# Six z_a and two z_b column blocks moved into block-product pairs, with index scores summed by adding DMAs, deferred low parts and ScalarE norm squares

## The chip, the cores and the metric

The kernel runs on one core of a Trainium2 chip. The metric is the device time of one execution in microseconds (us). The kernel before takes 1558.45 us, the median of 3 runs (1557.06 to 1560.39).

## The reference, cut to what matters

One layer of a hybrid block on 16 meta tokens and 512 tokens (528 columns), width 2048, all in fp32:

```python
proj = rms_norm(x, norm_g) @ w_in
q_a, k_a, v_a, z_a, q_i, k_i, w_i, q_b, f_b, i_b, z_b, gates = split(proj)
# branch A: index scores pick 128 keys per query, attention over these
score = einsum('bqhs,bqh->bqs', relu(qi @ ki), w_i)      # 16 index heads
sel   = top_k(where(admissible, score, -inf), 128)
o_a   = softmax(q @ k[sel] * d**-0.5) @ v[sel]           # 8 heads; q, k normed and rotated
y_a   = o_a * silu(z_a)
# branch B: gated linear recurrence over 8 heads
o_b   = hgrn2(silu(q_b), 1 - f, i_b, log(f))             # f from sigmoid(f_b)
y_b   = rms_norm(o_b) * silu(z_b)
# merge
out = x + sum_n(sigmoid(gates_n) * (y_n @ w_branch_n)) @ w_out
```

## The kernel before, in words

Activations lie transposed: 128 channels on the partitions, tokens along the row. An fp32 product is three fp32r matmuls on TensorE (PE): both factors are split into a high and a low part, and hi·hi, lo·hi and hi·lo are summed (`mm3`, and L90 and L92 in `mm`).

The projection is cut into column blocks of 128 channels. A **plain block** runs over 16 k tiles, 3 matmuls of 128x512 each: 48 matmuls into one PSUM bank, `pg`. A **pair** (`run_pair`) computes two blocks at once over four quarters of the weights (11, 12, 21, 22) and two halves of tokens, by seven block products instead of eight (`SEVEN`): each product has 8 k tiles and 3 matmuls of 256 columns (264 where meta tokens are needed), into the banks px, py, pz, pw. That is 7 x 24 = 168 matmuls for two blocks. The sums of weights for a pair are made by VectorE (DVE; `sum_1`, `sum_2`) and by two adding DMAs on GpSimd's queue (POOL; `sum_3`, `sum_4`, L115). The combinations of the products are made by DVE in p1, g1 and g2.

The order of blocks is the list `jobs`: k_i with w_i; 8 q_i; 8 z_a; 4 k_a; 4 v_a; 8 q_a; 6 z_b: 39 plain blocks. Then 29 pairs: 5 with q_b and the last two z_b, 8 of f_b with i_b (264 wide), 16 of gates. Then 32 blocks of the branch matmul (24 matmuls 128x512 each, and 768 in all for both branches' halves), then 8 pairs of the output matmul. The blocks of one kind hang together with tasks: 8 `idx_task` make the scores of 16 index heads (PE `psc`, relu on ScalarE (ACT) into `rl`, weighted sum on DVE, L127); 4 `topk_task` find the 128 largest by 16 rounds of MAX8 and MATCH_REPLACE8 (L682, L683); `ka_task`, `va_task` and `qa_task` norm, rotate and attend; `pv_task` ends a head and multiplies it by silu(z_a), read back from HBM (zad); `hgrn_task` runs one head of the recurrence at a time.

**What sets the order.** The program is written in the order in which Python issues it. A clock per engine is modelled (`Core.at`); between the main matmuls `pump` lets waiting tasks issue their next piece when the model says that what they wait for is there. Each engine then runs its own instructions in that order, and waits at the first one whose operands aren't there.

**Weights.** Each chunk of 1024 columns is loaded on SyncE's queue (SP, L362) into one of NRAW = 6 `raw` buffers, split by ACT (`wh`, L100) and DVE (`wl` = raw - wh, L106) into one of 3 buffers each, two chunks ahead of PE (`split_upto`). Both halves of the split are issued together in `hi_lo`; the load that refills a raw buffer is issued behind the last use of that buffer.

Of the kernel before, what the change touches and what calls it, by code (L numbers as in the profile page):

```python
# [37 lines left out]
LAT = 180.0  # L38
ROOM = 2
SAME = {"pe": 0.0, "act": 60.0, "dve": 125.0, "pool": 60.0}  # L40
MARGIN = 300.0
NSLOT = 69


class Core:
# [67 lines left out]

    def dma_add(self, out, a):
        self.nc.gpsimd.dma_start(out, a, accum_op=OP.add)  # L115
        return self.at("pool", 4000.0, [out], [out, a])
# [27 lines left out]
class Slots:  # L144
# [36 lines left out]
def hybrid_kernel(ctx, tc, x, meta, vecs, w_in, rows, w_branch, w_out,  # L181
# [64 lines left out]
    def bank(name):  # L246
        while len(B1.free) <= need[0]:
            yield WAIT
        return B1.get(name)

    def pair(name, keep=0):
        while len(B2.free) <= keep:
            yield WAIT
        return B2.get(name)
# [37 lines left out]
    masks = cp.tile([128, 7 * 256 + 512], U8, name="masks")  # L292
# [8 lines left out]
    def make_masks():  # L301
        mf = slot("mf")
        nc.sync.dma_start(mf[:, :448], masks_d)
        yield E.clk["pe"] + 3000.0
        for i in range(7):
            yield E.dve([masks], [mf], 256, lambda v: v.tensor_copy(
                masks[:, 256 * i:256 * i + 256].rearrange("p (c n) -> p c n", c=4),
                mf[:, None, 64 * i:64 * i + 64].to_broadcast([128, 4, 64])))
        yield E.dve([masks], [ident], 512, lambda v: v.tensor_copy(
            masks[:, 1792:2304].rearrange("p (c n) -> p c n", c=4), ident[:, None, :].to_broadcast([128, 4, 128])))  # L310
        S.put(mf)

# [39 lines left out]
    NRAW = 6  # L352
# [27 lines left out]
    def hi_lo(k, src, m):  # L380
        h = wp.tile([128, 1024], F32R, name=f"wh{k}", tag=f"wh{k % NWS}")
        l = wp.tile([128, 1024], F32R, name=f"wl{k}", tag=f"wl{k % NWS}")
        E.act(h[:, :m], src, AF.Copy)
        (E.ptt if k < 6 else E.tt)(l[:, :m], src, h[:, :m].bitcast(F32), OP.subtract)
        return h, l

    def split_chunk(k, ch):
        load_upto(ch["i"])
# [3 lines left out]
        if k < 4:  # L392
            for g in range(2):
# [19 lines left out]
    def sum_2(pr):  # L413
        if not hasattr(pr, "s2"):
            pr.s2 = wp.tile([128, 1024], F32, name=f"sum2_{pr.raw['11']['i']}", tag="s2")
            E.tt(pr.s2, pr.s1, pr.raw["11"]["raw"], OP.add)

    def sum_3(pr):
        if not hasattr(pr, "s3"):
            pr.s3 = pr.raw["21"]["raw"]  # L420
            E.dma_add(pr.s3, pr.raw["11"]["raw"])

    def sum_4(pr):
        if not hasattr(pr, "s4"):
            pr.s4 = pr.raw["12"]["raw"]
            E.dma_add(pr.s4, pr.s2)

    def prep_op(k, op):

        pr, nm = op["pair"], op["name"]  # L430
        first = pr.raw["11"]["i"]
        load_upto(first + (0 if nm == "11" else 2 if nm == "s2" else 3))
# [7 lines left out]
        h, l = hi_lo(k, src, 1024)  # L440
# [3 lines left out]
        used = {"s3": 2, "22": 3, "s4": 4}.get(nm)  # L444
        if used:
            load_upto(first + used - 1 + NRAW)

# [84 lines left out]
    def norm_rope(ps, p, ntab, tab, name):  # L532
# [6 lines left out]
        E.act(sv, ps, AF.Square)  # L539
        E.red(r[:, 0:4], sv)  # L540
# [3 lines left out]
        E.tt(yv, ps, r[:, 8:12, None].to_broadcast([p, 4, 128]), OP.mult)  # L544
# [13 lines left out]
    def ki_task(kw):  # L558
# [45 lines left out]
        for c0, n, v in ((0, 272, pb[:, 0, :272]), (272, 256, pb[:, 1, :256])):  # L604
            E.act(kkH[:, c0:c0 + n], v, AF.Copy)
            E.tt(kkL[:, c0:c0 + n], v, kkH[:, c0:c0 + n].bitcast(F32), OP.subtract)
        S.put(d, dm)
        B2.put(pb)
        kk.extend((kkH, kkL))

    score = []
    idx_left = [8]

    def idx_task(j, xq):
# [18 lines left out]
        if not score:  # L633
            score.extend(slots("score", 4))
        for i in range(2):
            hd = 2 * j + i
            for qt in range(4):
                kq = KQ[qt]
                lq = st_[i][:, 128 * qt:128 * qt + 128]
                if kq > 512:  # L640
                    pb = yield from pair("psc")
                    for c in range(2):
                        E.mm(pb[:, c, :264], lq, kkH[:, 264 * c:264 * c + 264], True, False)
                        e = E.mm(pb[:, c, :264], lq, kkL[:, 264 * c:264 * c + 264], False, True)
                    v = pb[:, :, :264]
                else:
                    pb = yield from bank("psc")
                    E.mm(pb[:, :kq], lq, kkH[:, :kq], True, False)
                    e = E.mm(pb[:, :kq], lq, kkL[:, :kq], False, True)
                    v = pb[:, :kq]  # L650
                yield e
                r = slot("rl")
                rv = r[:, :kq].rearrange("p (a b) -> p a b", a=2) if kq > 512 else r[:, :kq]
                E.act(rv, v, AF.Relu)
                (B2 if kq > 512 else B1).put(pb)
                sc = score[qt][:, :kq]
                w = wi[:, qt, hd:hd + 1]
# [15 lines left out]
    def topk_task(qt):  # L673
        kq = KQ[qt]
        sc = score[qt][:, :kq]
# [12 lines left out]
        S.put(ws, score[qt])  # L688
# [77 lines left out]

    zad = [tc.dram_tile([128, 512], F32, name=f"zad{h}") for h in range(8)]
    yd = [[tc.dram_tile([128, 512], F32, name=f"yd{n}_{h}") for h in range(8)] for n in range(2)]

    def spill(dst, s, e):  # L770
        yield e
        nc.sync.dma_start(dst, s[:, :512])
        S.put(s)

# [3 lines left out]
    def qa_task(h, xq, prev):  # L778
# [46 lines left out]
        for qt in (3, 2, 1, 0):  # L825
            kq = KQ[qt]
            xs = ps[qt] = slot("lg")
# [17 lines left out]
    def pv_task(h, ps, e):  # L845
# [10 lines left out]
        def turn(b):  # L856
# [6 lines left out]
            if b >= 0 and b < 3:  # L863
# [7 lines left out]
        for b in (3, -1, 0, 1, 2):  # L871
# [33 lines left out]
        e = E.tt(z[:, :512], po, z[:, :512], OP.mult)  # L905
        B1.put(po)
        spawn(spill(yd[0][h], z, e), 0)
# [11 lines left out]
    MT = cp.tile([128, 256], F32, name="MT")  # L919
    VM = [cp.tile([128, 16], F32, name=f"VM{i}") for i in range(2)]  # L920
    LB = []

    def lb_task():
        while not all(t.done for t in qa_tasks):
            yield WAIT
        LB.append((yield from pair("phl")))
        E.dve([LB[0]], [], 512, lambda v: v.memset(LB[0][:, 0], 0.0))

    def hgrn_task(h, prev):
# [6 lines left out]
        while not LB:  # L936
            yield WAIT
        while len(S.free) < 3:
            yield WAIT
        at = AT[0]  # L940
        mt, vt = MT, slot("vt")
        pm = LB[0][:, 1, :]
        pb = yield from bank("phv")
        E.tr(pm[:16, :128], VM[h % 2], ident)
# [13 lines left out]
        E.dve([at], [pb], 512, lambda v: v.copy_predicated(at[:, :512], masks[:, 1792:2304], pb))  # L958
# [5 lines left out]
        for li, m in enumerate(LEVELS):  # L964
            pb = LB[0][:, 0, 256 * (li % 2):256 * (li % 2) + 256]
# [4 lines left out]
            for c in range(4):  # L970
# [164 lines left out]
    def d_fb(h):  # L1135
        def f(g):
# [578 lines left out]
```

## Time and profile before

| | us |
|---|---|
| median of the runs | 1558.45 |
| the profiled execution | 1557.17 |
| its span, first to last instruction | 1555.4 |
| PE busy | 1536.8 (99%) |
| DVE busy | 1102.3 (71%) |
| ACT busy | 635.0 (41%) |
| POOL busy | 135.1 (9%) |
| the 16 DMA engines, queue q1 and q0 | 38.9% and 14.8% of the span |

Busy time is that of the profiled execution. A share of the whole span says little about one stage: the stages differ, and the views by window below give them apart. In the chain of work that ended last, each piece is followed back from the end of the program to what released it; what stands there is what the time is made of. In the views of single instructions the first two columns are the start and the duration in us, and the bracket is the idle time of the engine just before, with what ended it.

### The profile page before, as it was taken

To read this page: it belongs to the slowest core of one execution; us is meant where nothing else is said; L and a number is where in the kernel's file an instruction comes from. 1 tells how busy PE (TensorE), PEld (TensorE's weight loads), DVE (VectorE), ACT (ScalarE), POOL (GpSimd) and SP (SyncE) were. 2 spreads that over 40 slices of the span, in tenths; PEclk is the share of its full clock that TensorE was granted. 3 is DMA by queue.
4 is the path that set the end of the run, shared out by engine and by line. 5 is a ranking of instruction groups with operands and counts; after the bars stand their busy time and mean duration, and the time that the engine had idled before them with its cause. 6 is when DMAs were issued, how large, how long until landed. Compare 5 with 4: busy or idle time off the path is not lost.

```text
span 1555.4 us, 29048 instructions
## 1 busy us (share of the span) xinstructions
PE 1536.8 (99%) x11904; PEld 1417.1 (91%) x11904; DVE 1102.3 (71%) x1903; ACT 635.0 (41%) x997; POOL 135.1 (9%) x136
## 2 busy tenths in 40 slices
PE   7999999999999999999999999999999999999998
PEld 6888889998888799999999999999999888889998
DVE  6687898625677888677677767686767544778775
ACT  5555422334445453443444344434433332334332
POOL 3100000100000001101000000100000000002222
PEclk9999999999999999999999999999999999999999
DMA  9323343333223465766757676757666755448773
GB/s 261 82 68 82 108 115 109 83 82 86 84 82 109 117 156 129 181 153 155 178 144 170 150 171 149 170 138 175 153 173 159 234 177 149 136 137 219 210 209 93
DMA packets 293173, 223.00 MB, mean 143 GB/s; under 512 B 10356, under 2 KB 264832, under 8 KB 293040
## 3 DMA queue, kind: packets, MB, share of 16 engines
q1 hardware_dynamic: 275664, 173.88, 38.9%
q0 software_dynamic: 10720, 38.89, 14.8%
q10 hardware_dynamic: 6656, 8.39, 1.6%
q8 instruction: 93, 1.52, 0.4%
q14 instruction: 40, 0.33, 0.1%
HBM read 161.35 MB, written 20.97 MB: 117 GB/s over the span
## 4 chain that ended last, share of the span: by engine, by line
PE 96%; ACT 1%; DVE 1%; DMA 1%; issue 1%; POOL 0%; ACTq 0%; SPq 0%; DVEq 0%; POOLq 0%
PE pg L92 39%; PE pz L90 11%; PE py L90 11%; PE px L90 10%; PE po L90 10%; PE pw L90 5%; PE phl L92 1%; PE psc L92 1%; PE pho L92 1%; PE pov L90 1%; PE plg L92 1%; PE ppt L96 1%; PE phs L92 1%; PE px L96 1%; PE pqa L96 0%
## 5 line engine op out<-in xcount | busy, mean ns | idle before, releaser
L100 ACT ACTIVATE wh<-raw 128x1024 fp32r<-128x1024 f32 x291 | 308.4, 1060 | 485.2 <-PE pg L92 128.8
L106 DVE TENSOR_TENSOR wl<-raw,wh 128x1024 fp32r<-128x1024 f32 x289 | 356.7, 1234 | 191.9 <-ACT wh L100 188.6
L92 PE MATMUL pg<-hH,wh 128*128 128x512 f32 (+1 forms) x720 | 261.1, 363 | 0.0
L92 PE MATMUL pg<-hH,wl 128*128 128x512 f32 (+1 forms) x720 | 256.1, 356 | 0.0
L92 PE MATMUL pg<-hL,wh 128*128 128x512 f32 (+1 forms) x720 | 255.9, 355 | 0.0
L90 PE MATMUL po<-wh,mh 128*128 128x256 f32 x896 | 158.7, 280 | 0.5 <-DVE xq L106 0.5
L92 PEld LDWEIGHTS pg<-hH,wl 128*128 128x128 f32 x720 | 135.3, 188 | 21.0
L92 PEld LDWEIGHTS pg<-hH,wh 128*128 128x128 f32 x720 | 135.7, 189 | 16.6
L92 PEld LDWEIGHTS pg<-hL,wh 128*128 128x128 f32 x720 | 135.4, 188 | 16.0
L90 PEld LDWEIGHTS po<-wh,mh 128*128 128x128 f32 x896 | 137.7, 189 | 0.8 <-DVE xq L106 0.7
L100 ACT ACTIVATE wh<-sum 128x1024 fp32r<-128x1024 f32 x74 | 78.5, 1061 | 140.0 <-PE pw L90 52.2
L90 PE MATMUL px<-hH,wh 128*128 128x256 f32 (+1 forms) x464 | 134.3, 289 | 0.0
L90 PE MATMUL px<-hH,wl 128*128 128x256 f32 (+1 forms) x464 | 130.8, 282 | 0.0
L90 PE MATMUL px<-hL,wh 128*128 128x256 f32 (+1 forms) x464 | 130.5, 281 | 0.0
L90 PE MATMUL po<-wl,mh 128*128 128x256 f32 x448 | 125.9, 281 | 0.0
L106 DVE TENSOR_TENSOR wl<-sum,wh 128x1024 fp32r<-128x1024 f32 x74 | 96.7, 1307 | 33.4 <-ACT wh L100 33.3
L92 PE MATMUL pg<-yH,wh 128*128 128x512 f32 x256 | 101.0, 394 | 0.0
L92 PE MATMUL pg<-yH,wl 128*128 128x512 f32 x256 | 100.8, 394 | 0.0
L92 PE MATMUL pg<-yL,wh 128*128 128x512 f32 x256 | 100.6, 393 | 0.0
L90 PEld LDWEIGHTS px<-hH,wh 128*128 128x128 f32 x464 | 87.4, 188 | 0.6
L90 PEld LDWEIGHTS px<-hL,wh 128*128 128x128 f32 x464 | 87.3, 188 | 0.0
L90 PEld LDWEIGHTS px<-hH,wl 128*128 128x128 f32 x464 | 87.3, 188 | 0.0
(312 smaller groups left out, 3368.5 us busy)
## 6 DMA issues: line engine op xcount, KB each, us to landing
raw<-in_w_in_dram SPq DMA_DIRECT2D x192, 512.0 KB, 4.2
raw<-raw POOLq DMA_DIRECT2D x37, 512.0 KB, 5.3
raw<-sum POOLq DMA_DIRECT2D x37, 512.0 KB, 6.1
raw<-in_w_branch_dram SPq DMA_DIRECT2D x32, 512.0 KB, 4.5
raw<-in_w_out_dram SPq DMA_DIRECT2D x32, 512.0 KB, 4.3
gd<-g SPq DMA_DIRECT2D x32, 256.0 KB, 4.6
g<-gd SPq DMA_DIRECT2D x30, 256.0 KB, 2.9
x<-in_x_dram SPq DMA_DIRECT2D x16, 256.0 KB, 5.4
```

The source lines that it names most:

```text
L90: self.nc.tensor.matmul(out, lhsT, rhs, start=start, stop=stop, skip_group_check=True)
L92: self.nc.tensor.matmul(out, lhsT, rhs, start=start, stop=stop)
L96: self.nc.tensor.transpose(out, in_, ident)
L100: self.nc.scalar.activation(out, in_, f, **kw)
L106: self.nc.vector.tensor_tensor(out, a, b, op=op)
```

## The change

The numbers of plain z_a and z_b blocks become 2 and 4 (`NZA`, `NZB`). The other 6 z_a and 2 z_b go into pairs with the q_b, so that 31 plain blocks and 33 pairs are left. Heads 2 to 7 of the attention end before their z_a is there: `pv_task` copies o_a and stores it to HBM (`oad`), and a new `ya_task` loads it and multiplies when the pair with z_a is done.

The index heads' products are scaled on ACT in place, the relu of query tiles 1 and 0 is one instruction, and the heads are summed by 45 adding DMAs on POOL's queue into the tiles of head 0. In `norm_rope` (k_a, their meta columns, q_a) the squares are four ACT instructions with an accumulator and the scaling is four ACT instructions.

The low part of a split is no longer issued with the high part: `low()` waits in `lows`, and `flush` issues it when the model says that ACT's copy is done, or when the next products need it. NRAW goes from 6 to 5, and the number of 528-column work slots from 69 to 72. The recurrence's masks move from buffers of their own into one slot, `p1` in a pair goes away (g1 and g2 are combined in place), the reciprocals of a softmax become one instruction, and model costs of DMAs change.

```diff
+NZA, NZB = 2, 4
...
-NSLOT = 69
+NSLOT = 72
...
     def dma_add(self, out, a):
         self.nc.gpsimd.dma_start(out, a, accum_op=OP.add)
-        return self.at("pool", 4000.0, [out], [out, a])
+        e = self.at("pool", 1000.0, [out], [out, a]) + 4000.0
...
+    lows = []
+
+    def flush(k):
+
+        while lows and (lows[0][1] <= E.clk["pe"] or lows[0][0] <= k):
+            lows.pop(0)[2]()
+
     def pump(limit=3000.0):
+        flush(-1)
...
-    NRAW = 6
+    NRAW = 5
...
-        E.act(h[:, :m], src, AF.Copy)
-        (E.ptt if k < 6 else E.tt)(l[:, :m], src, h[:, :m].bitcast(F32), OP.subtract)
+        def low():
+            (E.ptt if k < 6 else E.tt)(l[:, :m], src, h[:, :m].bitcast(F32), OP.subtract)
+            load_upto(upto)
+
+        lows.append((k, E.act(h[:, :m], src, AF.Copy), low))
+        if k < 6:
+            flush(k)
         return h, l
 
     def split_chunk(k, ch):
+        flush(k - 2)
...
-        E.act(sv, ps, AF.Square)
-        E.red(r[:, 0:4], sv)
+        for b in range(4):
+            E.act(sv[:, b], ps[:, b], AF.Square, accum_out=r[:, b:b + 1])
...
-        E.tt(yv, ps, r[:, 8:12, None].to_broadcast([p, 4, 128]), OP.mult)
+        for b in range(4):
+            e = E.act(yv[:, b], ps[:, b], AF.Copy, scale=r[:, 8 + b:9 + b])
+        yield e
...
+                for qt in qts:
+                    e = E.act(r[:, o:o + KQ[qt]], r[:, o:o + KQ[qt]], AF.Copy, scale=wi[:, qt, hd:hd + 1])
+                    if hd == 0:
+                        score[qt] = r[:, o:o + KQ[qt]]
+                    o += KQ[qt]
                 if hd == 0:
-                    e = E.ts(sc, r[:, :kq], w, None, OP.mult)
+                    sums[qts] = r
                 else:
-                    e = E.stt(sc, r[:, :kq], w, sc, OP.mult, OP.add)
-                S.put(r)
+                    yield e
+                    E.dma_add(sums[qts][:, :o], r[:, :o])
+                    S.put(r)
...
+    def ya_task(h, s):
+
+        while h not in have_o or not S.free:
+            yield WAIT
+        o = slot("oa")
+        nc.sync.dma_start(o[:, :512], oad[h])
+        yield E.clk["pe"] + 5000.0
+        e = E.tt(o[:, :512], o[:, :512], s[:, :512], OP.mult)
+        S.put(s)
+        spawn(spill(yd[0][h], o, e), 0)
+        yield e
...
-        e = E.tt(z[:, :512], po, z[:, :512], OP.mult)
+        if h < NZA:
+            e = E.tt(z[:, :512], po, z[:, :512], OP.mult)
+            spawn(spill(yd[0][h], z, e), 0)
+        else:
+            e = E.act(z[:, :512], po, AF.Copy)
+            spawn(spill(oad[h], z, e, lambda: have_o.add(h)), 0)
...
+    for t in "iiiiiiiiaakkkkvvvvqqqqqqqqbbbb":
+        c, m, d = kinds[t]
+        jobs.append(Job("in", c + 128 * count[t], 128, m, done=d(count[t])))
...
-    Q, Z = ([(c + 128 * h, d(h)) for h in range(8)] for c, d in ((C_QB, d_qb), (C_ZB, d_zp)))
-    first = [(Z[6], Q[0]), (Z[7], Q[1]), (Q[3], Q[2]), None, (Q[5], Q[4]), None, (Q[7], Q[6]), None]
+    blocks2 = [(h, (C_QB + 128 * h, d_qb(h))) for h in range(8)]
+    blocks2 += [(h + 0.8, (C_ZB + 128 * h, d_zp(h))) for h in range(NZB, 8)]
+    blocks2 += [(0.4 + 6.0 * (h - NZA) / (8 - NZA), (C_ZA + 128 * h, d_zap(h))) for h in range(NZA, 8)]
+    blocks2.sort(key=lambda b: b[0])
```

The score sums on POOL's queue, at the start of the program. `rl` are the products of an index head (528 columns for query tile 3, 400 for tile 2, 416 for tiles 1 and 0 together), `kay` and `kis` the norms, `raw`, `wh` and `wl` the first chunks of the weights. In before:

```order
L110 TENSOR_TENSOR wl_740<-raw_215,wh_739 128x1024
L566 MEMSET kiy_803 128x320
L110 TENSOR_TENSOR kis_804<-kis_804,mhalf 128x5
L110 TENSOR_TENSOR kay_2587<-kay_2587,mhalf 128x4
L110 TENSOR_TENSOR kay_2735<-kay_2735,mhalf 128x4
```

The same place in after:

```order
L603 MEMSET kiy_796 128x320
L111 TENSOR_TENSOR kis_797<-kis_797,mhalf 128x5
L121 DMA rl_955<-rl_977 128x528
L121 DMA rl_955<-rl_999 128x528
L121 DMA rl_969<-rl_1002 128x400
L121 DMA rl_969<-rl_1024 128x400
L121 DMA rl_983<-rl_1045 128x416
L121 DMA rl_983<-rl_1064 128x416
```

POOL had nothing between the norm of k_i and that of k_a; it now has the adding DMAs, 15 into each of three tiles, one behind the other.

DVE where the first top-k begins, in after (`rl_983` holds the scores of tiles 1 and 0, `zs` is silu(z_a) of a plain block, `wl` the low part of a chunk):

```order
L107 TENSOR_TENSOR wl_1820<-raw_1496,wh_1819 128x1024
L107 TENSOR_TENSOR wl_1873<-raw_1575,wh_1872 128x1024
L718 MEMSET rl_983 64x64
L724 MAX m_0_1894<-rl_983 128x8
L725 MATCH_REPLACE tk_1893<-m_0_1894,rl_983 128x144
L107 TENSOR_TENSOR zs_1912<-pg_1818,zs_1912 128x512
L107 TENSOR_TENSOR wl_1918<-raw_1628,wh_1917 128x1024
L107 TENSOR_TENSOR wl_1972<-raw_1696,wh_1971 128x1024
```

In before, DVE's own sums of the scores (L127) stand ahead of that place:

```order
L106 TENSOR_TENSOR wl_1498<-raw_1120,wh_1497 128x1024
L127 SCALAR_TENSOR_TENSOR score_942<-rl_1521,tabs_98,score_942 128x144
L127 SCALAR_TENSOR_TENSOR score_943<-rl_1530,tabs_98,score_943 128x272
L127 SCALAR_TENSOR_TENSOR score_944<-rl_1539,tabs_98,score_944 128x400
L127 SCALAR_TENSOR_TENSOR score_945<-rl_1550,tabs_98,score_945 128x528
L106 TENSOR_TENSOR wl_1560<-raw_1176,wh_1559 128x1024
```

The score sums are gone from DVE; the MEMSET of `rl_983` waits for the last adding DMA into it, and the `wl` of the next chunks stand behind that MEMSET.

DVE in a pair of f_b and i_b, in before, from the low part of its s3 product to that of its s4 product (with numbers; `raw82` to `raw85` are the buffers of this pair, `raw86` to `raw88` and `sum1_86` belong to the next):

```order
L106 TENSOR_TENSOR wl88_5839<-raw83_5421,wh88_5838 128x1024
L106 TENSOR_TENSOR hz_444_5847<-g1_440_5681,hz_444_5847 128x512
L106 TENSOR_TENSOR p1_443_5837<-p1_443_5837,py_232_5850 128x264
L106 TENSOR_TENSOR wl89_5879<-sum1_82_5708,wh89_5878 128x1024
L106 TENSOR_TENSOR wl90_5907<-raw84_5599,wh90_5906 128x1024
L106 TENSOR_TENSOR p1_443_5837<-py_232_5850,p1_443_5837 128x264
L106 TENSOR_TENSOR sum1_86_5939<-raw87_5714,raw88_5842 128x1024
L106 TENSOR_TENSOR wl91_5942<-raw85_5601,wh91_5941 128x1024
```

The same place of a pair of f_b and i_b in after (`raw66` to `raw69` are its buffers, `raw70` to `raw72` the next pair's; `oa` is o_a of an attention head, `zs` silu(z_a)):

```order
L107 TENSOR_TENSOR wl72_5332<-raw67_5100,wh72_5331 128x1024
L107 TENSOR_TENSOR g1_408_5368<-g2_406_5330,py_208_5343 128x264
L107 TENSOR_TENSOR wl73_5372<-sum1_66_5200,wh73_5371 128x1024
L107 TENSOR_TENSOR oa_405_5307<-oa_405_5307,zs_404_5299 128x512
L107 TENSOR_TENSOR wl74_5401<-raw68_5102,wh74_5400 128x1024
L107 TENSOR_TENSOR g2_406_5330<-py_208_5343,g2_406_5330 128x264
L107 TENSOR_TENSOR sum1_70_5433<-raw71_5339,raw72_5341 128x1024
L107 TENSOR_TENSOR wl75_5436<-raw69_5173,wh75_5435 128x1024
```

The order in a pair stays, but for the multiplication of `oa`. With five raw buffers `raw72` takes the buffer of `raw67`, so that its load stands behind `wl72`, five instructions ahead of `sum1_70`, which reads it; in before `raw88` takes the buffer of `raw82`, which the adding DMA of s3 reads last, ahead of `wl88`.

## Rows read from the trace of the kernel before

**Rows 1.** The page of the profile: busy time of each engine, the granted clock of PE in 40 slices, and the chain of work that ended last, by engine.

```profile
PE 1536.8 (99%) x11904; PEld 1417.1 (91%) x11904; DVE 1102.3 (71%) x1903; ACT 635.0 (41%) x997; POOL 135.1 (9%) x136
...
PEclk9999999999999999999999999999999999999999
...
PE 96%; ACT 1%; DVE 1%; DMA 1%; issue 1%; POOL 0%; ACTq 0%; SPq 0%; DVEq 0%; POOLq 0%
```

**Rows 2.** The waits of PE over the whole span, the first two and the last of nine rows (14.7 us in all): line waited for, us in total, times, longest.

```profile
PE pc L96 <- DMA vrow<-in_vecs_dram: 8.2, 1, 8.2
PE phs L92 <- ACT MT L100: 2.6, 8, 1.3
...
PE pov L90 <- DVE pTL L106: 0.2, 1, 0.2
```

**Rows 3.** ACT's timeline: the first instruction behind three of the eight z_a blocks, the second being the next block and the third six blocks behind the first.

```profile
174.62 0.60 ACT L100 ACTIVATE zs<-pg 128x512 f32<-128x512 f32 x1 [0.65 <-PE pg L92]
...
185.86 0.60 ACT L100 ACTIVATE zs<-pg 128x512 f32<-128x512 f32 x1 [4.76 <-PE pg L92]
...
242.06 0.60 ACT L100 ACTIVATE zs<-pg 128x512 f32<-128x512 f32 x1 [4.80 <-PE pg L92]
```

**Rows 4.** The chain of work that ended last, pieces in order of time (start, us, what): the first and the last product of a 256-wide pair, the first of the pair behind it, and the branch matmul.

```profile
553.28 2.85 PE px L90 x24
...
570.30 2.83 PE pz L90 x24
573.14 2.92 PE px L90 x24
...
1214.86 177.81 PE pg L92 x768
```

**Rows 5.** Windows of the stages: index scores; z_a blocks; k_a and v_a; attention; the pair of rows 4; two pairs and a head of the recurrence. Columns: us, then busy us and count of PE, PEld, DVE, ACT and POOL, granted clock of PE, DMA share, GB/s.

```profile
70.00:165.00 95.00, 95.00 (x478) 80.73 (x477) 72.33 (x120) 52.56 (x98) 0.00 (x0) 1.00 0.27 73
174.00:242.00 68.00, 68.00 (x293) 54.65 (x292) 64.80 (x184) 15.63 (x18) 0.00 (x0) 1.00 0.45 124
254.00:356.00 102.00, 102.00 (x793) 98.58 (x793) 51.36 (x95) 34.98 (x78) 6.46 (x7) 1.00 0.31 83
356.00:553.00 197.00, 195.44 (x1003) 161.94 (x1002) 143.94 (x358) 92.69 (x182) 9.32 (x9) 1.00 0.35 95
553.00:573.00 20.00, 20.00 (x171) 19.95 (x170) 17.09 (x26) 11.81 (x20) 1.74 (x2) 1.00 0.77 172
594.00:664.00 70.00, 68.62 (x730) 67.04 (x729) 51.63 (x82) 27.97 (x40) 6.17 (x7) 1.00 0.66 158
```

**Rows 6.** Groups of instructions of the parts that the change edits: xcount, busy us, mean ns of one, idle before and its releaser.

```profile
L127 DVE SCALAR_TENSOR_TENSOR score<-rl,tabs,score 128x144 f32<-128x144 f32 (+3 forms) x60 | 32.1, 564 | 13.0 <-ACT rl L100 12.8
L682 DVE MAX8 m<-tk 128x8 f32<-128x144 f32 (+3 forms) x60 | 30.1, 502 | 0.0
L683 DVE MATCH_REPLACE8 tk<-m,tk 128x144 f32<-128x144 f32 (+3 forms) x60 | 29.5, 492 | 0.0
L106 DVE TENSOR_TENSOR wl<-raw,wh 128x1024 fp32r<-128x1024 f32 x289 | 356.7, 1234 | 191.9 <-ACT wh L100 188.6 <-DMA raw<-in_w_in_dram 1.5 <-DMA yd<-za 1.2
L132 DVE TENSOR_REDUCE qay<-qas 128x4 f32<-128x512 f32 x8 | 5.4, 677 | 1.1 <-ACT qas L100 1.1
L106 DVE TENSOR_TENSOR qay<-pqa,qay 128x512 f32<-128x512 f32 x8 | 5.5, 686 | 1.2 <-POOL qay L110 1.1
L100 ACT ACTIVATE rl<-psc 128x400 f32<-128x400 f32 (+3 forms) x64 | 27.2, 451 | 38.8 <-PE psc L92 38.6
L100 ACT ACTIVATE qas<-pqa 128x512 f32<-128x512 f32 x8 | 4.7, 589 | 1.7 <-PE pqa L96 1.7
L100 ACT ACTIVATE v<-pva 128x128 f32<-128x128 f32 x4 | 1.1, 277 | 5.6 <-DVE vL L106 5.6
L100 ACT ACTIVATION_READ_ACCUMULATOR lg<-lg,small 128x1 f32 x32 | 6.0, 187 | 0.0
L115 POOL DMA_DIRECT2D raw<-raw x37 | 31.9, 862 | 533.2 <-DVE sum L106 533.2
```

**Rows 7.** PE's timeline, the starts of the first matmuls of two successive q_i blocks, each with score matmuls behind it; and the page's list of DMA issues (KB each, us to landing).

```profile
139.24 4.88 PE pg L92 x21
...
153.06 4.89 PE pg L92 x21
...
raw<-in_w_in_dram SPq DMA_DIRECT2D x192, 512.0 KB, 4.2
raw<-raw POOLq DMA_DIRECT2D x37, 512.0 KB, 5.3
```

**Rows 8.** DVE's and SP's timeline and the chain in one 264-wide pair: the low part of the pair's s3 product, the load issued behind it, the sum for the next pair, the low part of its s4 product, and that product on PE.

```profile
758.09 1.23 DVE L106 TENSOR_TENSOR wl<-raw,wh 128x1024 fp32r<-128x1024 f32 x1 [1.08 <-ACT wh L100]
...
759.34 0.37 SPq L362 DMA_DIRECT2D raw<-in_w_in_dram  x1
...
766.20 1.21 DVE L106 TENSOR_TENSOR sum<-raw,raw 128x1024 f32<-128x1024 f32 x1
767.34 1.22 DVE L106 TENSOR_TENSOR wl<-raw,wh 128x1024 fp32r<-128x1024 f32 x1
...
771.65 2.92 PE pz L90 x24
```

More of the change, by code (lines that the diff above doesn't have):

```diff
@@ L164, in get, with when @@
         return a
+    def when(self):
+        return min(self.last[t][0] for t in self.free) + LAT
     def put(self, *aps):
@@ L246, in bank @@
     def bank(name):
-        while len(B1.free) <= need[0]:
+        while len(B1.free) <= need[0] or B1.when() > E.clk["pe"]:
             yield WAIT
@@ L251, in pair @@
     def pair(name, keep=0):
-        while len(B2.free) <= keep:
+        while len(B2.free) <= keep or B2.when() > E.clk["pe"]:
             yield WAIT
@@ L439, in prep_op @@
             src = {"s1": pr.s1, "s2": pr.s2, "s3": raw["21"], "s4": raw["12"]}[nm]
-        h, l = hi_lo(k, src, 1024)
+        used = {"s3": 2, "22": 3, "s4": 4}.get(nm, 0)
+        h, l = hi_lo(k, src, 1024, first + used - 1 + NRAW if used else -1)
         w = pr.ncols
@@ L632, in idx_task @@
         kkH, kkL = kk
-        if not score:
-            score.extend(slots("score", 4))
         for i in range(2):
             hd = 2 * j + i
[L637 to L650, printed above, removed]
+            for qts in ((3,), (2,), (1, 0)):
+                pb = yield from (pair if qts == (3,) else bank)("psc")
+                o = 0
+                for qt in qts:
+                    kq = KQ[qt]
+                    lq = st_[i][:, 128 * qt:128 * qt + 128]
+                    for c, n in ((0, 264), (1, 264)) if kq > 512 else ((0, kq),):
+                        out_ = pb[:, c, :n] if kq > 512 else pb[:, o:o + n]
+                        E.mm(out_, lq, kkH[:, n * c:n * c + n], True, False)
+                        e = E.mm(out_, lq, kkL[:, n * c:n * c + n], False, True)
+                    o += kq
@@ L687, in topk_task @@
         e = E.ts(bias[qt], w, BIAS, None, OP.mult)
-        S.put(ws, score[qt])
+        S.put(ws)
+        if qt > 1:
+            S.put(sums[qt,])
+        elif all(t.done for t in topk_tasks[:2] if t is not topk_tasks[qt]):
+            S.put(sums[1, 0])
         yield e
@@ L826, in qa_task @@
             kq = KQ[qt]
-            xs = ps[qt] = slot("lg")
+            xs = ps[qt] = slot("lg") if qt else ps[1][:, KQ[1]:KQ[1] + kq]
             f2 = (lambda a: a.rearrange("p (a b) -> p a b", a=2)) if kq > 512 else (lambda a: a)
@@ L925, in lb_task @@
             yield WAIT
-        LB.append((yield from pair("phl")))
-        E.dve([LB[0]], [], 512, lambda v: v.memset(LB[0][:, 0], 0.0))
+        lb = yield from pair("phl")
+        E.dve([lb], [], 512, lambda v: v.memset(lb[:, 0], 0.0))
+        LB.append(lb)
     def hgrn_task(h, prev):
@@ L935, in hgrn_task @@
         q, f, k, vx = (hg[h][i] for i in ("q", "f", "k", "v"))
-        while not LB:
+        while len(LB) < 2:
             yield WAIT
+        masks = HC[3]
         while len(S.free) < 3:
@@ L940, in hgrn_task @@
         at = AT[0]
-        mt, vt = MT, slot("vt")
-        pm = LB[0][:, 1, :]
+        mt, vt = HC[0], slot("vt")
+        lb = next(t for t in LB if t != 1)
+        pm = lb[:, 1, :]
         pb = yield from bank("phv")
-        E.tr(pm[:16, :128], VM[h % 2], ident)
+        E.tr(pm[:16, :128], HC[1 + h % 2], ident)
         for c in range(4):
@@ L1154, in f @@
         def f(g):
-            E.act(VM[h % 2].rearrange("p (a b) -> p a b", a=2), halves(g)[:, :, 0:8], AF.Copy)
+            if h == 0:
+                spawn(hgrn_consts(), 0)
+                while not HC:
+                    pump(1e9)
+            E.act(HC[1 + h % 2].rearrange("p (a b) -> p a b", a=2), halves(g)[:, :, 0:8], AF.Copy)
             hg[h]["v"] = g
@@ L1161, in f, with d_zap @@
             s = silu_mul(b, "hz")
-            hg.setdefault(h, {})["z"] = 1
-            spawn(spill(zd[h], s, E.clk["dve"] + LAT), 0)
+            spawn(spill(zd[h], s, E.clk["dve"] + LAT, z_there(h)), 0)
+        return f
+    def d_zap(h):
+        def f(g):
+            s, _ = silu(g, "zs")
+            spawn(ya_task(h, s), 1)
         return f
```

145 lines of the change are left out of this document (84 added, 61 removed).

## The prediction, before the run

> **What bounds the kernel now.** I read the page first: PE is busy 99% of the span, at the full granted clock in every slice, and 96% of the chain that ended last lies on PE [rows 1]. So the time is the sum of PE's matmuls and the few places where PE stands still. The waits of PE are 14.7 us in all, of which 8.2 come before the first matmul, so 6.5 us lie within the program [rows 2]. Then the windows by stage: DVE is at 95% beside the z_a blocks (64.80 of 68.00), and PE is nevertheless busy for the whole window; in the attention PE loses 1.56 us of 197 at 73% of DVE, and in two pairs with a head of the recurrence 1.38 of 70 [rows 5]. A stage can therefore be nearly full on DVE without any cost, as long as the order is right. What the change is worth is read from PE's work first, then from what new waits it makes.
>
> **Fewer matmuls.** Eight plain blocks (8 x 48 matmuls) go and four pairs (4 x 168) come. A plain block's price: from the first silu behind a z_a block to that six blocks on, 242.06 - 174.62 = 67.44 us, 11.24 each, or 234 ns per 512-wide matmul [rows 3]; PE is full there and holds little but these [rows 5]. A pair's: 573.14 - 553.28 = 19.86 us, or 118 ns per 256-wide matmul [rows 4]. So 8 x 11.24 = 89.9 us go and 4 x 19.86 = 79.4 come: **-10.5 us**. The branch matmul gives a second price, 177.81 / 768 = 231.5 ns [rows 4], 11.11 a block, and with it -9.4. I take the z_a blocks' own price, since they are what goes.
>
> The Trainium skill ("TensorE: Matmul & The Clock Gate", "Back-to-back issue gap") gives a sustained spacing of 81 ns at 128 columns and 131 ns at 512. By an estimate from it a block is 48 x 131 = 6.3 us, a pair at some 95 ns 16.0, and the change would add 4 x 16.0 - 8 x 6.3 = 13.6 us. The trace differs, with 234 and 118 ns at the full granted clock [rows 1, 3, 4]: here halving the columns halves the time, so I give this rule 1 in 100.
>
> **New pairs' other work.** Each needs two sums on DVE, and two adding DMAs and their issue on POOL. The pair of rows 4 has all this and PE is busy 20.00 of 20.00 us [rows 5]: 0. Loading and multiplying o_a adds one DVE instruction to six pairs, of 0.69 us by the nearest 512-wide row (`qay`) [rows 6]; DVE has 2.9 us free in such a pair [rows 5]: 0, and at most 6 x 0.69 = 4.1 if no gap were found.
>
> **The score stage.** DVE loses its sums, 60 x 0.564 us and a few more. ACT gains 64 scalings; priced like the relus, 27.2 us [rows 6], that makes 52.56 + 27.2 = 79.8 of 95 us, 84% [rows 5]. PE is the engine it serves, with the high parts and the relus; as DVE served at 95% elsewhere, I take 0. POOL, idle there [rows 5], gets 45 issues x 0.862 = 38.8 us [rows 6]. The adds into one tile follow each other at the pace of heads: two heads per q_i block, 153.06 - 139.24 = 13.82, so 6.91 us a head; a 512 KB adding DMA lands in 5.3 us [rows 7] and these are half as large. So the sums keep up, and the last is there at most 3 x 0.862 + 5.3 = 7.9 us behind the last product. The first MEMSET of the top-k waits for it, with silu(z_a) and the next two `wl` queued behind it on DVE; the two `wl` ahead of it hold PE busy for one block, 11.24 us. 0, with 3.3 us to spare.
>
> **k_a, v_a and attention.** The top-k (30.1 + 29.5 = 59.6 us of DVE [rows 6]) loses six z_a blocks as its cover and runs beside two of them and the k_a and v_a. Estimate of DVE there: 64.80 + 51.36 [rows 5], less 12 `wl` at 1.234, 6 silu products at 0.686 and 5 norms at 0.677 + 0.686 [rows 6], so 116.2 - 25.8 = 90.4 us in 68 + 102 - 67.4 = 102.6, 88%. It was 95% without loss, but without chains in which PE waits for DVE's results; k_a and v_a have them. The norms on ACT: four squares with their accumulator reads and four scalings, 4 x (0.277 + 0.187) + 4 x 0.277 - 0.589 = 2.4 us more on ACT and 1.36 less on DVE each [rows 6], 13 times. ACT has two thirds of that stage free [rows 5]; the chain of one norm gets longer by about 1 us, which delays what waits on it in a task and not PE, which meanwhile has main matmuls. The attention has two z_b blocks fewer beside it, and its DVE share stays: (143.94 - 8 x 1.36 - 4 x 1.234) / (197 - 22.5) = 73%. Cost of the thinner cover, bounded by the nearest rows: all 6.5 us of waits within the program [rows 2] could go (-6.5), and the k_a and v_a could lose what the pairs with a head lose, 2% (1.38 of 70), some +2, or several times that. I take **+1**, since nothing of the old waits is touched.
>
> **Five raw buffers and late low parts.** The load that the next pair's `sum1` reads now waits for the low part of s3. In one pair that ends at 759.32 and the issue stands at 759.34 [rows 8]; with a landing of 4.2 us [rows 7] the data are there at 763.5; the sum starts at 766.20: 2.7 us to spare, and the low part of s4 behind it ends 3.1 us before its product (768.56 against 771.65) [rows 8]. So 0. The deferred low parts fill idle time of DVE, of which 188.6 us stand in front of `wl` waiting for ACT [rows 6]; as DVE isn't the bound, 0 too. Masks, reciprocals, p1 and the slot number touch only DVE and memory: 0.
>
> **The sum**, against the profiled execution's 1557.17: 1557.17 - 10.5 + 1.0 = 1547.7. The median of the runs, 1558.45, stands 1.3 above it, so the forecast for the median is **1549.0**, in its own range of 1545 to 1553.5 (below: 3 us of the old waits gone and none new; above: the cheaper block price and 3.5 us more of new waits).
>
> **Rivals.**
> - *A thin cover (0.15).* Top-k pieces stand in front of what the k_a and v_a chains need, and PE, in order, waits at their transposes. For it: DVE goes from 50% to an estimated 88% there [rows 5]. Against it: the modelled clocks place the tasks, and at 95% nothing was lost. Eight tasks with some three hand-overs each, every one late by one MAX8 of 0.5 us [rows 6], make 12 us at the most and half of it likely, on top of the forecast: 1554 to 1561.
> - *Sums that don't keep up (0.06, slower).* If an adding DMA takes longer than a head's 6.91 us, the lag grows 15 times, and DVE stands at the top-k's MEMSET with the `wl` behind it. With t per add PE loses about 15 x (t - 6.91) + t + 1.7 - 11.2. It decides against the change from t = 7.9 us (13 us lost); at 8 us, 1564. Against it are the 5.3 us for twice the bytes [rows 7]; for it, that three tiles' adds share POOL's queue with an issue of 0.86 us each. The Trainium skill ("SBUF — State Buffer", "SBUF: two separate sides") says that a DMA issued from GpSimd can't write its descriptors while VectorE holds the port that they share, and tells of 620 ns becoming 3100. By it an add could take 5.3 + 2.5 = 7.8 us. The issues of before took 862 ns with DVE at 74 to 85% [rows 5, 6], so the trace shows no such stop.
> - *Five buffers too few (0.03, slower).* The slack of 2.7 + 3.1 us is gone when a load takes over 10 us. It decides from 0.33 us in each of 33 + 8 pairs (13.5 us): 1562. Against it: 4.2 us of mean landing [rows 7].
> - *PE prices other than by columns (0.01)*, as above: 1572. *Waits that go (0.03)*, all 6.5 us of them and none new: 1541.5 to 1545. *Anything else, slower (0.02).*
>
> **Chances and range.** The forecast has 0.70. Within 0.2% (3.1 us, about what a measurement of this kernel can tell from no change) means 1555.3 to 1561.6. Faster: 0.70 + 0.03 + a third of the thin cover, 0.05: 0.78. The same: the other two thirds, 0.10, and 0.01 of slow sums or buffers: 0.11. Slower: the rest, 0.11. The range is 1545.0 to 1557.0: it holds 0.70 and over half of the thin cover, about 0.79.
>
> **What the profile of after would show.** Right: PE groups with 384 fewer 512-wide and 672 more 256-wide matmuls, the same prices per block, PE at 99% with under 8 us of waits past the start. The thin cover: waits of PE for DVE in the k_a and v_a, or `wl` late. Slow sums: DVE idle before the MEMSET of `rl`, released by a DMA, and PE waiting for `wl` in the first z_a block. Too few buffers: `sum` released by the DMA of `raw` in each pair, and PE waiting at pz. The forecast is wrong if the windows of k_a and v_a or of the scores show PE below 98%.

## The result, and the profile after

The changed kernel takes 1547.64 us (median of 6 runs, 1547.29 to 1550.38) against 1557.53 before (median of 6 runs, the three above among them): a ratio of 0.9937, 95% interval 0.9925 to 0.995, 9.9 us less. The forecast was 1549.0, a range of 1545.0 to 1557.0. The profiled execution took 1549.21 us. It has a low granted clock near its start (0.67 from 18 to 20 us and 0.50 from 20 to 22), which the profiled execution of before hasn't (1.00), so its span, 1547.4, is 8.0 shorter and not 9.9.

The page of after, where [rows 1] stand for before, and all the waits of PE, for [rows 2]:

```profile
PE 1528.8 (99%) x12192; PEld 1426.8 (92%) x12192; DVE 1077.0 (70%) x1823; ACT 699.7 (45%) x1210; POOL 183.0 (12%) x189
```

```profile
PE pc L97 <- DMA vrow<-in_vecs_dram: 8.1, 1, 8.1
PE pho L93 <- DVE S L137: 2.4, 1, 2.4
PE phs L93 <- ACT hc L101: 2.1, 6, 1.1
PE pg L93 <- POOL el L111: 0.8, 1, 0.8
PE px L97 <- DVE xm L130: 0.7, 1, 0.7
PE po L91 <- DVE xq L107: 0.5, 1, 0.5
PE phl L93 <- DVE QA L107: 0.3, 1, 0.3
```

The waits within the program other than for S fell from 6.5 us to 4.4, and a large one is new: 2.4 us in which `pho`, of a recurrence head, waits for S, the head's state. The chain shows the matmuls' prices again (start, us, what; for [rows 4]): the last plain block behind the attention, the first products of the first and the second pair, and the branch matmul.

```profile
450.87 11.92 PE pg L93 x51
462.79 2.85 PE px L91 x24
...
482.69 2.92 PE px L91 x24
...
1206.64 178.04 PE pg L93 x768
```

11.92 / 51 is 234 ns, and 482.69 - 462.79 = 19.90 us a pair. Up to the first pair the program is 553.28 - 462.79 = 90.5 us shorter, for 89.9 us of plain blocks removed; the pairs' stage is 1206.64 - 462.79 = 743.9 us against 661.6, 82.3 longer, where four pairs are 79.4. That stage lost 2.8 us more than it gained elsewhere.

The windows of the same stages (columns as in [rows 5]):

```profile
70.00:165.00 95.00, 95.00 (x475) 80.49 (x475) 42.44 (x70) 78.47 (x138) 35.25 (x41) 1.00 0.88 175
190.00:290.00 100.00, 100.00 (x776) 96.55 (x775) 93.29 (x247) 41.91 (x131) 6.06 (x7) 1.00 0.31 85
290.00:462.00 172.00, 171.95 (x905) 143.30 (x904) 121.02 (x308) 100.60 (x262) 10.89 (x9) 1.00 0.31 85
1024.00:1028.00 4.00, 4.00 (x36) 4.00 (x36) 2.41 (x3) 1.52 (x3) 0.00 (x0) 1.00 1.07 244
1028.00:1032.00 4.00, 1.94 (x17) 1.75 (x16) 0.66 (x2) 1.15 (x2) 0.00 (x0) 1.00 0.60 184
1032.00:1036.00 4.00, 3.65 (x18) 3.65 (x19) 2.68 (x6) 0.60 (x1) 0.00 (x0) 0.57 0.30 88
```

The first three are the scores, the k_a and v_a blocks and the attention: PE loses nothing in the first two and 0.05 us in the third, with VectorE at 93% in the second. The last three hold the new wait. VectorE's and SP's timeline there:

```profile
1021.16 4.22 SPq L387 DMA_DIRECT2D raw<-in_w_in_dram  x2
1025.43 1.17 SPq L835 DMA_DIRECT2D oa<-oad  x1
...
1031.35 0.69 DVE L107 TENSOR_TENSOR oa<-oa,zs 128x512 f32<-128x512 f32 x1 [4.94 <-DMA oa<-oad]
1031.95 1.10 DVE L137 SCALAR_TENSOR_TENSOR S<-S,TT,phs 128x128 f32<-128x128 f32 x3
```

The load of o_a of head 7 is issued behind two `raw` loads that waited on SP's queue, and lands 5.8 us later (the six such loads take 2.0 to 8.0 us, where the program's model allows 5). VectorE, in order, stands 4.94 us at the multiplication, S is queued behind it, and PE stops. In the stretch behind it the granted clock is 0.57 of full speed, which is 1.2 GHz for most of it, another (1 - 0.57) x 4 = 1.7 us.

### The profile page after: what moved, and what is told of

Its sections match the earlier page's. It is cut to its first block, busy times and chain, and to the rows that moved or that the text cites. A ratio compares the mean times of both kernels' runs of the same rounds, so it can differ in the third digit from the quotient of the medians.

```text
span 1547.4 us, 29924 instructions
## 1 busy us (share of the span) xinstructions
PE 1528.8 (99%) x12192; PEld 1426.8 (92%) x12192; DVE 1077.0 (70%) x1823; ACT 699.7 (45%) x1210; POOL 183.0 (12%) x189
## 4 chain that ended last, share of the span: by engine, by line
PE 97%; DMA 1%; ACT 1%; issue 1%; DVE 0%; POOL 0%; ACTq 0%; SPq 0%; DVEq 0%; POOLq 0%
PE pg L93 34%; PE pz L91 12%; PE py L91 12%; PE px L91 12%; PE po L91 10%; PE pw L91 6%; PE phl L93 1%; PE psc L93 1%; PE pov L91 1%; PE plg L93 1%; PE pho L93 1%; PE ppt L97 1%; PE px L97 1%; PE phs L93 1%; PE pqa L97 1%
## 5 line engine op out<-in xcount | busy, mean ns | idle before, releaser
L93 PE MATMUL pg<-hH,wh 128*128 128x512 f32 (+1 forms) x592 | 210.8, 356 | 0.0
L93 PE MATMUL pg<-hL,wh 128*128 128x512 f32 (+1 forms) x592 | 205.5, 347 | 0.0
L93 PE MATMUL pg<-hH,wl 128*128 128x512 f32 (+1 forms) x592 | 205.4, 347 | 0.0
L91 PE MATMUL px<-hH,wh 128*128 128x256 f32 (+1 forms) x528 | 151.6, 287 | 0.0
L91 PE MATMUL px<-hH,wl 128*128 128x256 f32 (+1 forms) x528 | 148.8, 282 | 0.0
L91 PE MATMUL px<-hL,wh 128*128 128x256 f32 (+1 forms) x528 | 148.5, 281 | 0.0
L93 PEld LDWEIGHTS pg<-hH,wl 128*128 128x128 f32 x592 | 111.3, 188 | 15.1
L93 PEld LDWEIGHTS pg<-hH,wh 128*128 128x128 f32 x592 | 111.5, 188 | 11.3
L93 PEld LDWEIGHTS pg<-hL,wh 128*128 128x128 f32 x592 | 111.4, 188 | 10.6
L91 PEld LDWEIGHTS px<-hL,wh 128*128 128x128 f32 x528 | 99.4, 188 | 0.1
```

Source lines behind the costliest of these rows:

```text
L91: self.nc.tensor.matmul(out, lhsT, rhs, start=start, stop=stop, skip_group_check=True)
L93: self.nc.tensor.matmul(out, lhsT, rhs, start=start, stop=stop)
```

## The experiments

Times are medians; each was compared with runs of the kernel before on the same chip, whose medians were 1557.4 to 1557.8.

**z_undo: the blocks back, the other edits kept.**

```diff
-NZA, NZB = 2, 4
+NZA, NZB = 8, 6
...
-    for t in "iiiiiiiiaakkkkvvvvqqqqqqqqbbbb":
+    for t in "iiiiiiiiaaaaaaaakkkkvvvvqqqqqqqqbbbbbb":
```

> All other edits of the change stay; the six z_a and two z_b blocks are plain blocks again (39 plain blocks, 29 pairs, with q_b and z_b paired in another order than before). Columns theory (the gain is 8 x 11.24 - 4 x 19.86 = 10.5 us of matmuls, the other edits are worth nothing by themselves): 1547.6 + 10.5 = 1558, within 2 us of the kernel before; and as all z_a are plain, no o_a is reloaded, so the wait of 2.4 us and the low clock behind it are gone, which takes some 4 us off again: 1554 to 1558. Rival (the gain comes from the sums on DMA, the late low parts and the norms): stays near 1548.

1555.18 us, ratio 0.9985 (0.9976 to 0.9994). The gain hangs on the blocks. The other edits together are worth 2 us here, where all blocks are plain again, in which PE's waits past the start are 3.7 us instead of 6.5.

**oa_late: the reloaded o_a multiplied later.**

```diff
-        yield E.clk["pe"] + 5000.0
+        yield E.clk["pe"] + 14000.0
```

> As the changed kernel, but the multiplication of a reloaded o_a is issued 14 instead of 5 us of modelled time behind its load. If the 4.94 us in which VectorE stood at that multiplication (head 7, load 6 us late on its queue) set PE's wait of 2.4 us and the low granted clock behind it (0.57 over 4 us, 1.7 us), 4.1 us are saved: 1543.5. Rival: the wait only moves to another place in that recurrence head, or the slot that is held longer makes another wait: 1546 to 1548.

1543.6 us, ratio 0.9914 (0.9901 to 0.9928): the wait for S is gone from PE's list, and 4.0 us with it. Against z_undo, which has no such wait either, the blocks are worth 11.6 us, for 10.5 by the two prices (the profiled executions, with spans of 1552.3 and 1541.8 us, are 10.5 apart).

**all_edits_back: the blocks in pairs without the relief.**

```diff
-        for b in range(4):
-            E.act(sv[:, b], ps[:, b], AF.Square, accum_out=r[:, b:b + 1])
+        E.act(sv, ps, AF.Square)
+        E.red(r[:, 0:4], sv)
...
-        for b in range(4):
-            e = E.act(yv[:, b], ps[:, b], AF.Copy, scale=r[:, 8 + b:9 + b])
-        yield e
+        E.tt(yv, ps, r[:, 8:12, None].to_broadcast([p, 4, 128]), OP.mult)
...
-                    e = E.act(r[:, o:o + KQ[qt]], r[:, o:o + KQ[qt]], AF.Copy, scale=wi[:, qt, hd:hd + 1])
...
+                        e = E.stt(score[qt], rv, w, score[qt], OP.mult, OP.add)
...
-                    yield e
-                    E.dma_add(sums[qts][:, :o], r[:, :o])
...
-        lows.append((k, E.act(h[:, :m], src, AF.Copy), low))
-        if k < 6:
-            flush(k)
+        E.act(h[:, :m], src, AF.Copy)
+        low()
```

> The blocks stay in pairs as in the changed kernel; the score sums go back to VectorE, the norms' squares and scalings too (as before), and the low part of a split is issued at once. Columns theory: PE does not wait for these, 1547.6 within 2 us. Relief theory (without these edits VectorE is too full beside the k_a and v_a blocks, where it is busy 93.3 of 100 us after the change): about 7 us more work of VectorE there for the norms, so over 100%, and PE waits for low parts or transposes: 1552 to 1560.

1555.13 us, ratio 0.9981 (0.9972 to 0.999): 7.5 us lost, as the relief theory has it. The place was not the one named, though: beside the k_a and v_a VectorE is busy 90.9 of 100 us, not over 100%, and PE loses nothing there; it stops at the end of the attention. The two windows:

```profile
190.00:290.00 100.00, 100.00 (x772) 96.38 (x771) 90.91 (x219) 33.59 (x74) 6.02 (x8) 1.00 0.31 85
...
440.00:480.00 40.00, 34.16 (x188) 28.90 (x187) 33.38 (x62) 20.40 (x40) 1.82 (x2) 0.91 0.28 76
```

In the second, 5.8 us are without work and 40 x 0.09 = 3.6 us are lost by the low clock. The last plain block was over before the last head was, and the first pair waited for what VectorE and ScalarE had left to do for it: the sums of tokens (`tr`, `tT`), which stand on VectorE behind the last head's `pTL`, and its weights. In the chain, whose last row is the pair's third product:

```profile
464.17 0.79 PE pov L91
...
467.76 0.42 DVE pTL L107
468.18 1.59 DVE tr L107 x3
...
475.10 1.99 ACT wh L101 x2
477.41 3.10 PE px L91 x24
```

**The three edits one by one.** Edits as in the diff above, each alone: norms_dve the first (with the scaling on VectorE), scores_dve the second (without the scaling on ScalarE), lows_now the third.

norms_dve:

> As the changed kernel, with the squares' sum and the scaling of the norms back on VectorE: 13 x 1.36 = 17.7 us more on VectorE, 11 of them beside the q_a blocks. If the end of the attention is set by VectorE's load, it comes up to 11 us later, of the 11.9 us that the last plain block gives: near the edge, 1547 to 1553. If the hand-over between the engines counts more than VectorE's load, the chain of one norm is 1 us shorter and nothing is lost: 1546 to 1548.

lows_now:

> As the changed kernel, with each low part issued at once behind its high part, so that VectorE stands at it until ScalarE's copy is done (188.6 us of such idle time before the change, 108.1 after). If this idle time is what made the attention end late in the run with the three edits back, this alone gives 1552 to 1556. If not: 1547.6 within 2 us.

scores_dve:

> As the changed kernel, with the score sums back on VectorE (the 45 adding DMAs and the 64 scalings on ScalarE are gone). With the three edits back the attention ended too late and the last plain block was over before it. If it is the score sums that matter, this alone gives most of the 7.5 us: 1552 to 1556. Columns theory for this edit (VectorE has room in the score stage, and the top-k's first instruction, which stood 7.02 us for the last adding DMA, starts earlier): 1547.6 within 2 us.

norms_dve took 1559.48 us (1.0007, 0.9998 to 1.0017), outside both of its expectations; lows_now 1553.27 (0.9965, 0.9952 to 0.9979), and scores_dve 1546.53 (0.9926, 0.9913 to 0.994). The two that lose are those in which the last head ends late (`za`, the copy of o_a, first and last start); the end of the top-k is shown beside it (`bias`). In after:

```profile
L130 DVE TENSOR_SCALAR bias<-tk x4: 234/402/481, 231.3 to 290.7; 128x144 bf16<-128x144 f32 x1, 128x272 bf16<-128x272 f32 x1, 128x400 bf16<-128x400 f32 x1, 128x528 bf16<-128x528 f32 x1
L101 ACT ACTIVATE za<-pov x6: 576/599/601, 358.4 to 450.9; 128x512 f32<-128x512 f32 x6
```

In norms_dve, and its window where the attention ends:

```profile
L130 DVE TENSOR_SCALAR bias<-tk x4: 235/334/435, 248.9 to 307.3; 128x144 bf16<-128x144 f32 x1, 128x272 bf16<-128x272 f32 x1, 128x400 bf16<-128x400 f32 x1, 128x528 bf16<-128x528 f32 x1
L101 ACT ACTIVATE za<-pov x6: 578/592/601, 382.7 to 466.9; 128x512 f32<-128x512 f32 x6
...
440.00:480.00 40.00, 34.04 (x191) 28.60 (x190) 34.45 (x66) 21.98 (x43) 1.75 (x2) 0.91 0.29 73
```

The top-k ends 16.6 us later and the attention 16.0 later, 4 us more than the 11.9 that the last plain block gave. In lows_now the two ends are 304.6 and 465.7, and in the window from 440 to 480 us PE is without work for 4.2 us at a mean clock of 0.96. The 11.9 us weren't all to spare, either: in after VectorE makes the last sums of tokens for the first pair in them, and ends 2.5 us before the product that reads them first begins (VectorE's timeline, then the chain):

```profile
462.09 1.05 DVE L107 TENSOR_TENSOR tT<-tr,tT 128x528 fp32r<-128x528 f32 x2
...
465.63 2.84 PE py L91 x24
```

Why the attention ends late stays open. That the k_a norms, some 7 us of VectorE, delay the top-k by 16.6 isn't explained by their duration, and norms_dve also drops the `yield` behind the scaling, which changes the order in which pieces are issued; no run tells the two apart. Nor does the end of the top-k decide by itself: in all_edits_back it ends 4.2 us earlier than in after, and the last head 18.2 us later.

```profile
L130 DVE TENSOR_SCALAR bias<-tk x4: 234/336/435, 228.1 to 286.5; 128x144 bf16<-128x144 f32 x1, 128x272 bf16<-128x272 f32 x1, 128x400 bf16<-128x400 f32 x1, 128x528 bf16<-128x528 f32 x1
L101 ACT ACTIVATE za<-pov x6: 573/586/598, 385.1 to 469.1; 128x512 f32<-128x512 f32 x6
```

The prices don't add up, either: the three edits undone together lose 7.5 us, the norms alone 11.8. A part of that is the wait of PE for S, which all_edits_back doesn't have and which is 3.2 us in norms_dve, with a granted clock of 0.50 from 1042 to 1046 us behind it. In scores_dve the top-k ends 18 us earlier, the attention where it ended in after (449.2), and the time is 1 us below that of after:

```profile
L130 DVE TENSOR_SCALAR bias<-tk x4: 234/336/435, 218.2 to 272.5; 128x144 bf16<-128x144 f32 x1, 128x272 bf16<-128x272 f32 x1, 128x400 bf16<-128x400 f32 x1, 128x528 bf16<-128x528 f32 x1
```

**more_zb and more_a: another pair, from two more z_b or from the last two z_a** (both with oa_late's edit, and the string of `jobs` changed to match).

```diff
-NZA, NZB = 2, 4
+NZA, NZB = 2, 2
```

```diff
-NZA, NZB = 2, 4
+NZA, NZB = 0, 4
```

more_zb:

> As oa_late, and two more z_b blocks go from plain blocks into a pair (29 plain blocks, 34 pairs). Columns theory: 2 x 11.24 - 19.86 = 2.6 us less than oa_late: 1540.9. Thin-cover theory: the attention, with two plain blocks fewer beside it, does not end ahead of the pairs or makes PE wait, and the 2.6 us or more are given back: 1543 to 1550.

more_a:

> As oa_late, with the last two plain z_a blocks moved into a pair too (29 plain blocks, 34 pairs, as many as with two more z_b). Columns theory: 1543.6 - 2.6 = 1541. If what decides is the time from the end of the top-k to the end of the plain blocks, the attention keeps its cover here, but the top-k has 22.5 us less, and q_a's logits wait for it, so that the attention ends later by up to that: then as with two more z_b, 1553 to 1556.

1554.95 us (0.998, 0.9971 to 0.9989), more than either expectation of more_zb, and 1552.69 (0.997, 0.9959 to 0.998): they lose 11 and 9 us against oa_late where the columns alone would save 2.6. The cover behind the attention was 11.9 us, and two blocks are 22.5. The windows around the end of the attention in more_zb, then those of more_a beside the k_a and v_a and at the end of the attention, and more_a's chain before the third product of the first pair:

```profile
290.00:440.00 150.00, 148.18 (x790) 123.89 (x789) 104.77 (x279) 90.73 (x253) 11.30 (x9) 1.00 0.28 78
440.00:480.00 40.00, 34.27 (x245) 32.04 (x246) 31.49 (x54) 20.64 (x36) 2.56 (x3) 0.91 0.47 115
...
190.00:290.00 100.00, 97.10 (x677) 89.49 (x676) 90.51 (x236) 40.63 (x124) 6.21 (x7) 1.00 0.30 81
440.00:480.00 40.00, 36.67 (x260) 34.19 (x258) 29.93 (x49) 20.39 (x34) 2.56 (x3) 0.91 0.51 122
...
446.99 0.61 ACT za L101
...
447.61 0.32 SPq L820
...
448.02 5.28 DMA raw<-in_w_in_dram
```

In more_a PE also stops 2.9 us at the transposes of the first q_a (2.1) and of the meta tokens' k_a (0.8), the kind of place that the rival of the thin cover named. Behind the attention a load of weights for the first pair stands on SP's queue behind the store of the last head's o_a, which waits for ScalarE's copy.

**more_a_scores and scores_oa: more_a with the score sums on VectorE, and the same without the extra pair.**

scores_oa:

> The score sums back on VectorE and the late multiplication of a reloaded o_a together. If the two are independent: 1546.5 less the wait of 2.0 us for S that was in the run with the sums alone, and the low clock behind it, together some 4 us: 1542.5. If not, 1543.6 (as the late multiplication alone) or above.

more_a_scores:

> The last two plain z_a in a pair, the score sums on VectorE, the late multiplication. If what spoiled the run without the score sums was the top-k's end (it set the first logits, 22.5 us of cover being gone), VectorE's sums bring that end 18 us forward (272.5 against 290.7 us), the attention ends ahead of the pairs again, and the columns count: 1542.5 - 2.6 = 1540. If what spoiled it was VectorE's load beside the attention itself: 1549 to 1553, as before.

scores_oa took 1544.84 us (0.9912, 0.9898 to 0.9926), with about the ratio of oa_late: 1.7 us less than the sums alone, which had 2.0 us of wait for S and, in their profile, no low clock behind it. The gains of the two edits don't add up, then. more_a_scores **1540.26** (0.9888, 0.9874 to 0.9902), 7.4 us faster than the change. In it the attention ends 14.7 us ahead of the first pair, which starts at 440.09, and PE loses next to nothing beside the k_a and v_a (99.98 of 100 us):

```profile
L130 DVE TENSOR_SCALAR bias<-tk x4: 236/334/436, 215.5 to 276.0; 128x144 bf16<-128x144 f32 x1, 128x272 bf16<-128x272 f32 x1, 128x400 bf16<-128x400 f32 x1, 128x528 bf16<-128x528 f32 x1
L101 ACT ACTIVATE za<-pov x8: 575/598/602, 298.6 to 425.4; 128x512 f32<-128x512 f32 x8
```

**raw4: four raw buffers** (`NRAW = 4`).

> As the changed kernel, with four raw buffers instead of five. The load of the next pair's fourth-last quarter then waits for the low part that stands just ahead of the sum that reads it, so that VectorE stands there some 3 us in each pair; the low part behind it ends about 0.6 us after its product could begin. If the ring has the spare time that was worked out (2.7 + 3.1 us with five buffers), this goes just beyond it: 33 to 41 times 0.6 us and more, 1560 to 1600. If transfers have more spare than that: 1547.6 within 3 us.

1634.7 us (1.0495, 1.0479 to 1.0512), 87 us lost, 2.1 in each of 41 pairs: more than expected. VectorE waits 89.5 us for `raw` from w_in at the sums:

```profile
DVE sum L107 <- DMA raw<-in_w_in_dram: 89.5, 32, 4.9
```

With five it is 6.5 us in 8 waits, none of which reaches PE. So five buffers leave enough spare time, and four don't.

**two_adds1: the sum of tiles 1 and 0 as two adding DMAs per head.**

```diff
-                        E.dma_add(sums[qts][:, :o], r[:, :o])
+                        E.dma_add(sums[qts][:, :272], r[:, :272])
+                        E.dma_add(sums[qts][:, 272:o], r[:, 272:o])
```

> As the changed kernel, but the sum for query tiles 1 and 0 is two adding DMAs per head instead of one. The last of them releases the top-k's first instruction, which stood 7.02 us with one add per head. If an add has to land before the next into the same tile is issued (5 us each, 10 per head against a head's 6.91): the sums lag by 15 x 3 = 46 us and PE stops for some 40 of them: 1575 to 1595. If the two halves travel side by side: 1547 to 1551.

1548.16 us (0.9936, 0.9918 to 0.9955): the two parts, of 136 and 72 KB, travel side by side (POOL issues up to four adds in 3.48 us, and they land 4.8 us behind their issue, in the median), and the top-k's first instruction waits 7.1 us as in after. What an add may cost before the sums lag was therefore not reached.

## Why the prediction was right, and where it wasn't

- **Fewer matmuls, -10.5:** right. Both prices came again in the trace of after (234 ns, and 19.90 us a pair), and z_undo against oa_late gives 11.6. The spacings of the Trainium skill ("TensorE: Matmul & The Clock Gate", "Back-to-back issue gap"), by which the change was estimated 13.6 us slower, are shown by no run here. Of the 1.4 us between the forecast and the result 0.9 are the median of before, 1558.45 in the first three runs and 1557.53 in six.
- **Net waits, +1:** near the truth as a sum, by luck: about 2 us of old waits went (z_undo), and a new one of 4 us came, and I had foreseen neither. I said that nothing of the old waits is touched, which was wrong, and costed the reload of o_a at 0 because VectorE had room. It had; the load was issued late on SP's queue and took 5.8 us, and S was behind the multiplication. I hadn't asked what is queued behind the instruction that waits.
- **Norms on ScalarE and late low parts, 0:** the step that failed. Undone, they cost 11.8 and 5.6 us against the changed kernel. I argued that VectorE isn't the bound; but the attention must end before the plain blocks run out, and it ended only 11.9 us ahead. The z blocks were its cover, and with these two edits the attention ends early enough without them. That the total was right all the same is luck as to this step: I priced at nothing what kept the thin cover from costing several us. By which order of pieces the two edits do it isn't shown.
- **The thin cover (rival, 0.15):** it didn't come, but a thin cover is what the undone edits, more_zb and more_a show, in the main at another place: the end of the attention. Beside the k_a and v_a VectorE at 93% (estimated 88%) cost nothing, and transposes there cost something only in more_a (2.9 us) and in two_adds1 (1.2).
- **Score sums:** they kept up, and are worth nothing by themselves (scores_oa against oa_late). VectorE stood 7.02 us for the last one:

```profile
179.08 0.11 DVE L718 MEMSET rl<- 64x64 f32 x1 [7.02 <-DMA rl<-rl]
```

That is 8.7 us behind the last product (its end at 170.37), where I had put at most 7.9, and PE lost nothing by it. ScalarE was at 83% for 84%. Half the bytes bought little: 264 KB land in 4.0 to 5.0 us (the medians of the runs), 512 KB in 4.8 and 5.3. The warning of the Trainium skill ("SBUF — State Buffer", "SBUF: two separate sides") of 620 ns becoming 3100 shows in no issue here: one took 948 ns in the mean and 1516 at the most, with VectorE at 45% there.

- **Five buffers:** right that they hold; with four the price was 2.1 us a pair.

## What to carry to other kernels

When a share of the bounding engine's work moves, price it by its rows, and then look at what that work was covering: a chain that ends just before its cover ends has at most that margin, and edits that look free on an idle engine may be what keeps it. Sum such a margin up before moving the next block. Here the edit that looked like a relief, the sums by DMA, ended the top-k 18 us later, and with it the next pair costs 9 us, while with the older sums on VectorE it saves 4.6 (1540.26 against 1544.84). Where an instruction waits for a DMA, name the queue that the DMA is issued on, what stands ahead of it there, and what stands behind the instruction.

## What was not expected of the hardware

- A wait of PE can cost almost twice its length: behind 2.4 us without work the granted clock of the next 4 us was 0.57, 1.2 GHz for most of it. The length doesn't tell: at the same place the clock stayed at 1.00 behind 2.0 us in scores_dve and 3.0 us in two_adds1, and was 0.50 behind 3.2 us in norms_dve. In two_adds1, the wait and the windows around its end:

```profile
1033.21 0.49 PE L93 MATMUL pho<-S,QA 128*128 128x128 f32 x2 [2.99 <-DVE S L137]
...
1032.00:1034.00 2.00, 0.79 (x7) 0.79 (x8) 1.73 (x5) 0.00 (x0) 0.00 (x0) 1.00 0.11 42
1034.00:1036.00 2.00, 2.00 (x20) 2.00 (x19) 1.76 (x3) 0.63 (x2) 0.00 (x0) 1.00 0.27 97
```

- The time of an adding DMA on POOL's queue hardly goes by its bytes: the medians are 5.3 and 4.8 us for the two of 512 KB in a pair and 5.0 for 264 KB in after (4.0 to 4.9 in other runs), and 4.8 for 136 KB and for 72 KB in two_adds1, whose two parts ran beside each other.
